# Twenty weight slabs split into their parts on ScalarE and VectorE instead of by a second transfer, and one activation table loaded at another place

## The chip, the cores and the metric

The kernel runs on one core of one Trainium2 chip, as one launch. The metric is the device time in microseconds (us) of one execution. A core has TensorE (PE, matrix products into PSUM), VectorE (DVE), ScalarE (ACT), GpSimd (POOL), SyncE (SP), and 16 DMA engines that move data between HBM and the on-chip SBUF. Each engine works through its own queue of instructions in the order in which the program wrote them; semaphores make one engine wait for another. Transfers are issued here from two queues, POOL's and SP's.

## The reference

Two layers of an encoder trunk on x of 512 tokens by 1024 features, all in float32:

```python
def reference(x, positions, attn_norm_g, w_in, ..., w_out, ffn_norm_g, w_gate, w_up, w_down):
    ...
    for l in range(DEPTH):                                   # DEPTH = 2
        h = rms_norm(x, attn_norm_g[l])
        z = jnp.einsum('bsd,dc->bsc', h, w_in[l])
        qa, ka, va, qb, kb, vb, ga, gb = jnp.split(z, IN_SPLITS, axis=-1)
        ...
        ya = jnp.einsum('bsc,cd->bsd', window_gqa(qa, ka, va, sink_a[l]), w_proj_a[l])
        ...
        yb = jnp.einsum('bsc,cd->bsd', neighbourhood_attn(qb, kb, vb, rel_bias_b[l]), w_proj_b[l])
        mixed = jax.nn.sigmoid(ga) * ya + jax.nn.sigmoid(gb) * yb
        x = x + jnp.einsum('bsd,de->bse', mixed, w_out[l])
        h = rms_norm(x, ffn_norm_g[l])
        u = jax.nn.silu(jnp.einsum('bsd,df->bsf', h, w_gate[l])) * jnp.einsum('bsd,df->bsf', h, w_up[l])
        x = x + jnp.einsum('bsf,fd->bsd', u, w_down[l])
    return x
```

w_out is 1024 by 1024, w_gate and w_up are 1024 by 2816.

## The kernel before

**Products in three parts.** A float32 operand is split into a high part in the reduced type `F32R` and a low part (what the rounding left). A product of two such operands takes three matrix products: high by high, high by low, low by high. Such a group of three with 512 columns is one unit of the program's own measure of progress (`UNIT`, L421); `pos` (L422) counts the progress of PE in it, and `at_pos` (L425) puts a piece of work at a position, where `tick` (L431) emits it between the matrix products.

**Weights** come in slabs. A slab of 512 rows by 256 columns lies on 128 partitions as 4 by 256 elements. `slab` (L443) books two steps for each: `w_load` (L504), 23 before its first use, a transfer on POOL's queue that rounds on the way and so leaves the high part; and `w_low` (L513), 15 before its use, where ACT writes the negated high part into the buffer of the low part and a second transfer from the same weights, also on POOL's queue, adds the weights onto it. `plan_pair` (L450) books the slabs of a pair of output blocks; `pair_matmul` (L798) takes them and runs the products.

**A layer** (`layer`, L1087) runs the input projections, 16 attention heads as chains of small steps between the products of the gates, the projections w_proj_a and w_proj_b (sigmoid gates before them), then w_out in four pairs, the leading 256 columns of w_gate and of w_up as one ordinary pair each, then five blocks ("quads") of 512 columns of w_gate and w_up by a Strassen scheme of seven products (m = 1, 5, 6, 2, 7, 3, 4), mixed with w_down.

**From w_out to the first quad.** `evac_x` (L1332) adds a finished block of w_out's product to x. After the second block of a pair it calls `Norm.chunk` (L763) for two blocks: on ACT the scaled high part and the square, on DVE the low part (`scalar_tensor_tensor`) and the running sum of squares. When the sum over all eight blocks is there, `Norm.chain` (L773) has PE sum it over the partitions (four tiny products with a vector of ones, "at<-ones" in the trace), DVE makes the inverse root (`rsqrt`, L744), PE spreads it ("at<-cst,rstd") and DVE copies it out as `rows`. `chain_x` (L1361) then scales x by it (eight `scalar_tensor_tensor`), makes the seven combinations of halves of x, and splits each: `high` on ACT, `low` on DVE. Meanwhile PE runs the leading pair of w_gate and of w_up, whose results are scaled by `rows`: `evac_g` (L1414) applies silu on ACT, `evac_u` (L1420) multiplies and splits. After the quad's products m = 1 and m = 5, product m = 6 goes on adding in a PSUM bank which `seed` (L1480) fills with the result of m = 1, by a copy on ACT (the trace's "ACT mm").

The quads' own weights are loaded raw, once, on SP's queue (`Quad.load`, L547), and split by ACT (`high`, L560) and DVE (`low`, L576); for the first w_gate quad most low parts are made by transfer (`low_by_transfer`, L533: ACT negates, a transfer adds).

**Who fixes the order.** The program is run twice. The first run is dry: it prices each instruction (`cost`, L274; DVE: elements by 1.04 or 0.52 ns and 0.075 us) and keeps a clock for each engine. A chain goes on when its `Need` (L355) is met by these clocks; `backlog` says how far the engine's clock may be ahead of PE's, and chain_x asks for 6.0 (`XLOG`, L34). The decisions and the places of all buffers in two arenas (one for float32, one for `F32R`) are kept, and the second run emits the program in that order. The dry run's clocks are no measurement; they set an order.

Of the kernel before, what the change touches and what calls it, by code (L numbers as in the profile page):

```python
# [12 lines left out]
F32 = mybir.dt.float32  # L13
F32R = mybir.dt.float32r
I32 = mybir.dt.int32
AF = mybir.ActivationFunctionType
ALU = mybir.AluOpType
AX = mybir.AxisListType

P = 128  # L20
# [5 lines left out]
KD = D // P  # L26
# [187 lines left out]
def trunk(ctx: ExitStack, tc: tile.TileContext, a: dict, out: bass.AP, lay: Layout):  # L214
# [20 lines left out]
    def buf(shape, dtype=F32):  # L235

        n = int(np.prod(shape))
        x = lay.place(n, dtype)
        t = arenas[dtype][:, x : x + n]
        if len(shape) == 2:  # L240
            t = t.rearrange("p (a b) -> p a b", b=shape[1])
        elif len(shape) == 3:
            t = t.rearrange("p (a b c) -> p a b c", b=shape[1], c=shape[2])
        return t
# [29 lines left out]
    def cost(eng, name, o, aps):  # L274
        n = max(x.free_size() for x in aps) / 1000.0
        in_psum = any(x.space == PS for x in aps[1:])
        if eng == "pe":
            cols = aps[2].free_size()
            if name == "transpose":
                return 0.1  # L280
            if aps[1].dtype == F32:
                return max(4 * cols, 256) / 2400.0 + 0.002
            return 0.12 if cols == 256 else (cols if cols >= 256 else 4 * cols) / 2255.0
        if eng == "act":
            return n * 0.833 + (0.06 if in_psum else 0.1) + 0.093 * sum(x.free_size() == 1 for x in aps[2:])
        if eng == "dve":
            fast = name in ("tensor_copy", "tensor_scalar") and not in_psum
            return n * (0.52 if fast else 6.4 if name == "reciprocal" else 1.04) + 0.075
        return n * 2.2 + 0.1

    steps = [0]
# [42 lines left out]
    V = Engine(nc.vector, "dve")  # L334
    A = Engine(nc.scalar, "act")
    G = Engine(nc.gpsimd, "pool")
    Q = Engine(nc.sync, "dma")
# [45 lines left out]
    def spawn(gen, after=None):  # L383
        c = [gen, Need()]
        if after is None:
            chains.append(c)
        else:
            chains.insert(chains.index(after) + 1, c)
        return c
# [32 lines left out]
    pos = [0.0]  # L422
    due = []

    def at_pos(t, f):  # L425
        bisect.insort(due, (t, len(seq), f))
        seq.append(0)

    seq = []

    def tick(dt):  # L431
        pos[0] += dt
        while due and due[0][0] <= pos[0]:
            due.pop(0)[2]()
# [3 lines left out]

    plan = []
    LEAD_H, LEAD_L, LEAD_RAW, LEAD_PREP = 23.0, 15.0, 14.0, 6.5  # L440
    total = [0.0]

    def slab(n, width, src, units, later_h=0.0, later_l=0.0):  # L443
        i = len(plan)
        plan.append((n, width, src))
        at_pos(total[0] - LEAD_H + later_h, lambda: w_load(i))
        at_pos(total[0] - LEAD_L + later_l, lambda: w_low(i))
        total[0] += units * UNIT

    def plan_pair(w, col, parts, row0=0):  # L450
        for k0 in range(0, parts, 4):
            n = min(4, parts - k0)
            r = row0 + P * k0
            slab(n, 256, [(0, w[r : r + P * n, col : col + 256])], 2 * n)

    def plan_token(w, cols):
        for k0 in range(0, KD, 2):
            at, src = 0, []
            for c, n in cols:
                src.append((at, w[P * k0 : P * k0 + 2 * P, c : c + n]))  # L460
                at += n
            slab(2, 512, src, 8)
# [6 lines left out]
    def ffn_steps():  # L469
        groups = [(0, 2)] + [(2 + 4 * i, 4) for i in range(QUADS)]  # L470
        steps = []
        for q in range(QUADS):
            ms = [("m", q, w, m) for w in ("w_gate", "w_up") for m in ORDER]
            ds = [("d", *groups[q], c) for c in range(KD)]
            for i, m in enumerate(ms):
                steps.append(m)
                if ds and i >= (1 if q else 5):
                    steps.append(ds.pop(0))
        return steps + [("d", *groups[-1], c) for c in range(KD)]
# [1 line left out]
    quads = {}  # L481

    def plan_ffn(l):
        plan_pair(a["w_gate"][l], 0, KD)
        plan_pair(a["w_up"][l], 0, KD)
        for step in ffn_steps():
            if step[0] == "m":
                _, q, w, m = step
                if m == ORDER[0]:
                    t = total[0]  # L490
                    early = 18.0 if q == 0 and w == "w_gate" else 0.0
                    quads[l, q, w] = Quad(a[w][l], 256 + 512 * q, t - early, early > 0.0)
                quads[l, q, w].due(m, total[0] - early)
                early = max(0.0, early - 1.2)
                total[0] += 24 * 0.12
            else:
                _, f0, n, c = step
                if c % 2 == 0:
                    slab(n, 256, [(0, a["w_down"][l][P * f0 : P * (f0 + n), P * c : P * c + 256])], 0, 3.0, 2.0)
                total[0] += n * UNIT  # L500

    highs, lows, used = {}, {}, [0]

    def w_load(i):  # L504

        if i not in highs:
            n1, n2, src = plan[i]
            highs[i] = buf([n1, n2], F32R)
            for at, ap in src:
                n = ap.shape[1]  # L510
                GQ.dma_start(highs[i][:, :, at : at + n], ap.rearrange("(k p) n -> p k n", p=P))

    def w_low(i):  # L513

        if i not in lows:
            n1, n2, src = plan[i]
            lows[i] = buf([n1, n2], F32R)
            A.activation(lows[i], highs[i].bitcast(F32), AF.Copy, scale=-1.0)
            for at, ap in src:
                n = ap.shape[1]  # L520
                GQ.dma_start(
                    lows[i][:, :, at : at + n], ap.rearrange("(k p) n -> p k n", p=P), accum_op=ALU.add
                )
# [61 lines left out]
    for l in range(DEPTH):  # L585
        w_in = a["w_in"][l]
        plan_token(w_in, [(QA0, 512)])
        plan_pair(w_in, KA0, KD)
        plan_token(w_in, [(QB0, 256), (KB0, 256)])
        plan_token(w_in, [(VB0, 512)])  # L590
        plan_token(w_in, [(QB0 + 256, 256), (KB0 + 256, 256)])
        for c in range(4):
            plan_pair(w_in, GA0 + 256 * c, KD)
        for c in range(ZB_AHEAD):
            plan_pair(w_in, GB0 + 256 * c, KD)
        for c in range(4):
            if c >= ZB_AHEAD:
                plan_pair(w_in, GB0 + 256 * c, KD)
            plan_pair(a["w_proj_a"][l], 256 * c, 4)
            plan_pair(a["w_proj_b"][l], 256 * c, 4)  # L600
        for c in range(4):
            plan_pair(a["w_out"][l], 256 * c, KD)
        plan_ffn(l)

    def gsplit(src, hi, lo, scale=None, eng=None):
# [26 lines left out]
    ones = cp.tile([P, 2], F32, tag="ones", name="ones")  # L632
# [4 lines left out]
    warm = cp.tile([P, 2], F32, tag="warm", name="warm")  # L637
# [449 lines left out]
    def layer(l):  # L1087
# [252 lines left out]


        last = l == DEPTH - 1
        spawn(nrm.chain())
        tail = []

# [87 lines left out]
        yield from pair_matmul(KD, nrm.xh, nrm.xl, evac_u)  # L1433

        gs = {}

        def soon(f, after=0.1):
            at_pos(pos[0] + after, f)

        def quadrant(q, w, i, t, src, sign):  # L1440

            if w == "w_gate":
                g = gs[i, t] = act()
                A.activation(g, src, AF.Silu, scale=sign)
                return
            hs, ls = us[q][i]
            g = gs[i, t]
            if sign > 0:
                V.tensor_tensor(g, src, g, ALU.mult)
            else:  # L1450
                V.scalar_tensor_tensor(g, src, sign, g, ALU.mult, ALU.mult)
            at = slice(256 * t, 256 * t + 256)
            g3 = g.rearrange("p (j n) -> p j n", j=2)
            A.copy(hs[:, :, at], g3)
            soon(lambda: V.tensor_tensor(ls[:, :, at], g3, hs[:, :, at].bitcast(F32), ALU.subtract), 1.0)
# [4 lines left out]
        def m_step(q, w, m):  # L1460
# [31 lines left out]
            def seed_c():  # L1492
                ps["c"] = plus(mm_bank())

            soon({
                1: seed,
                5: fetch,
# [34 lines left out]
        for i, step in enumerate(steps_[:-KD]):  # L1532
            if step[0] == "m":
                _, q, w, m = step
                yield f"x{l}{m}"
                yield from m_step(q, w, m)
            else:
                _, f0, n, c = step
                if c % 2 == 0:
                    wk = w_take()  # L1540
                o = mm_bank()
                yield from d_products(o, c, range(f0, f0 + n), wk, True, True)
                soon(lambda c=c, o=o: add_x(c, o))
        if not last:
            norms[2 * l + 2] = Norm(2 * l + 2)
        _, f0, n, _ = steps_[-1]
# [46 lines left out]
```

## Time and profile before

| what | value |
|---|---|
| median of 3 runs (lowest, highest) | 1441.97 us (1440.86, 1449.07) |
| the profiled execution | 1444.73 us |
| its span, first to last instruction | 1442.9 us |
| mean granted TensorE clock | 0.993 |
| ACT busy, DVE busy | 706.8 us, 912.2 us |
| moved by DMA | 221.10 MB |

The profile is of one execution. All instructions carry one line of the source (L308, the helper that emits them), so they are told apart by what they write and read: "mm" and "at" are PSUM banks, "arena" is any buffer of the two arenas, in_w_up and the like are the weights in HBM. A row of a timeline gives start, duration, engine, operation, operands and count; the bracket at its end is how long the engine stood idle before it, and what ended the wait. Rows of one kind that follow each other are merged; two such instructions on DVE or ACT overlap by some 0.1 us.

### The profile page before, as it was taken

To read this page: it belongs to the slowest core of one execution; us is meant where nothing else is said; L and a number is where in the kernel's file an instruction comes from. 1 tells how busy PE (TensorE), PEld (TensorE's weight loads), DVE (VectorE), ACT (ScalarE), POOL (GpSimd) and SP (SyncE) were. 2 spreads that over 40 slices of the span, in tenths; PEclk is the share of its full clock that TensorE was granted. 3 is DMA by queue.
4 is the path that set the end of the run, shared out by engine and by line. 5 is a ranking of instruction groups with operands and counts; after the bars stand their busy time and mean duration, and the time that the engine had idled before them with its cause. 6 is when DMAs were issued, how large, how long until landed. Compare 5 with 4: busy or idle time off the path is not lost.

```text
span 1442.9 us, 20988 instructions
## 1 busy us (share of the span) xinstructions
PE 1394.6 (97%) x8074; PEld 1224.6 (85%) x8074; DVE 912.2 (63%) x1752; ACT 706.8 (49%) x1191; POOL 363.4 (25%) x370
## 2 busy tenths in 40 slices
PE   5999999999989999999999999999998999999998
PEld 3778888888779999999987788888887999999997
DVE  3977777543667565665648768783448666574753
ACT  3476766643454343433544776574346343343431
POOL 4533222233221111101244322223232120111110
PEclk9999999999999999999999999999998999999999
DMA  9977788799865645645699678888996674736555
GB/s 226 170 159 129 140 161 157 142 196 259 146 139 144 156 117 143 155 112 117 134 201 174 132 129 155 160 158 155 260 206 109 147 175 116 178 89 145 121 100 117
DMA packets 209316, 221.10 MB, mean 153 GB/s; under 512 B 25900, under 2 KB 177632, under 8 KB 209216
## 3 DMA queue, kind: packets, MB, share of 16 engines
q0 software_dynamic: 157808, 165.13, 61.3%
q1 hardware_dynamic: 51408, 54.62, 13.3%
q8 instruction: 64, 1.05, 0.3%
q14 instruction: 36, 0.29, 0.1%
HBM read 207.13 MB, written 2.10 MB: 145 GB/s over the span
## 4 chain that ended last, share of the span: by engine, by line
PE 77%; DVE 12%; issue 3%; DMA 3%; ACT 3%; POOL 1%; DVEq 0%; POOLq 0%; ACTq 0%
PE mm L308 60%; PE at L308 18%; DVE arena L308 9%; ACT arena L308 3%; DVE sm L308 3%; DMA arena<-in_w_in 2%; DMA arena<-in_w_up 1%; POOL arena L308 1%; DMA cst<-in_consts 1%; DVE hf L308 0%; DVE den L308 0%; ACT L308 0%; ACT mm L308 0%; ACT sm L308 0%; DVEq L308 0%
## 5 line engine op out<-in xcount | busy, mean ns | idle before, releaser
L308 PE MATMUL mm<-arena 128*128 128x512 f32 (+1 forms) x5568 | 1123.6, 357 | 20.7 <-ACT mm L308 12.5
L308 PEld LDWEIGHTS mm<-arena 128*128 128x128 f32 x5568 | 907.1, 191 | 150.3 <-ACT mm L308 12.9
L308 ACT ACTIVATE arena<-arena 128x1024 fp32r<-128x1024 f32 (+3 forms) x276 | 232.7, 862 | 188.8 <-DMA arena<-in_w_down 58.9
L308 ACT CAST arena<-arena 128x1024 fp32r<-128x1024 f32 (+2 forms) x250 | 212.0, 864 | 220.9 <-DVE arena L308 218.5
L308 PE MATMUL at<-arena 128*128 128x256 f32 (+2 forms) x1952 | 303.8, 296 | 5.0 <-DVE arena L308 3.5
L308 PEld LDWEIGHTS at<-arena 128*128 128x128 f32 x1952 | 265.7, 191 | 25.9 <-DVE arena L308 8.1
L308 DVE TENSOR_TENSOR arena<-arena,arena 128x1024 fp32r<-128x1024 f32 (+2 forms) x240 | 233.0, 984 | 59.7 <-ACT arena L308 59.3
L308 DVE TENSOR_TENSOR arena<-arena,mm 128x512 f32<-128x512 f32 x144 | 98.7, 686 | 248.4 <-PE mm L308 248.3
L308 POOL DMA_DIRECT2D arena<-in_w_in x168 | 168.3, 1368 | 339.3 <-ACT arena L308 329.5
L308 POOL DMA_DIRECT2D arena<-in_w_down x96 | 98.2, 1218 | 502.1 <-ACT arena L308 357.5
L308 DVE TENSOR_TENSOR arena<-arena 128x1024 f32<-128x1024 f32 (+3 forms) x196 | 158.3, 823 | 4.0 <-ACT arena L308 1.5
L308 DVE TENSOR_TENSOR arena<-at,arena 128x384 fp32r<-128x384 f32 (+4 forms) x206 | 114.4, 562 | 49.6 <-ACT arena L308 42.2
L308 ACT CAST arena<-at 128x384 fp32r<-128x384 f32 (+2 forms) x164 | 74.4, 459 | 117.2 <-PE at L308 99.9
L308 PE MATMUL at<-cst,arena 128*128 128x128 f32 x504 | 85.9, 277 | 9.7 <-DVE arena L308 5.7
L308 PEld LDWEIGHTS at<-cst,arena 128*128 128x128 f32 x504 | 64.3, 142 | 26.8 <-DVE arena L308 6.8
L308 ACT ACTIVATE arena<-arena,negm 128x256 f32<-128x256 f32 (+1 forms) x128 | 71.4, 559 | 6.5 <-DVE negm L308 5.7
L308 DVE TENSOR_TENSOR arena<-mm,arena 128x512 f32<-128x512 f32 x72 | 49.3, 686 | 33.7 <-PE mm L308 33.6
L308 ACT COPY arena<-at 64x512 f32<-64x512 f32 (+1 forms) x60 | 34.9, 582 | 69.8 <-PE at L308 68.5
L308 POOL DMA_DIRECT2D arena<-in_w_out x32 | 35.1, 1287 | 60.5 <-ACT arena L308 60.5
L308 DVE CUSTOM_DVE_ANT_0 arena<-at,cst,nsnk 128x256 f32<-128x256 f32 (+1 forms) x64 | 34.4, 546 | 18.0 <-PE at L308 17.7
L308 DVE CUSTOM_DVE_ANT_0 arena<-at,arena 128x256 f32<-128x256 f32 (+1 forms) x64 | 30.7, 484 | 15.0 <-PE at L308 14.6
L308 DVE TENSOR_SCALAR arena<-arena,sm 128x384 f32<-128x384 f32 (+1 forms) x102 | 33.9, 387 | 1.1
(70 smaller groups left out, 436.4 us busy)
## 6 DMA issues: line engine op xcount, KB each, us to landing
arena<-in_w_in POOLq DMA_DIRECT2D x104, 512.0 KB, 7.2
arena<-in_w_down POOLq DMA_DIRECT2D x80, 512.0 KB, 6.7
arena<-in_w_gate SPq DMA_DIRECT2D x20, 1024.0 KB, 7.5
arena<-in_w_up SPq DMA_DIRECT2D x20, 1024.0 KB, 5.3
arena<-in_w_in POOLq DMA_DIRECT2D x64, 256.0 KB, 6.3
arena<-in_w_out POOLq DMA_DIRECT2D x32, 512.0 KB, 8.4
arena<-in_w_proj_a POOLq DMA_DIRECT2D x16, 512.0 KB, 7.0
arena<-in_w_proj_b POOLq DMA_DIRECT2D x16, 512.0 KB, 5.9
```

What stands on the lines that cost most here:

```text
L308: f(*args, **kw)
```

## The change

Three things change.

1. The 8 slabs of w_out and the 2 of the leading pair of w_gate, in each layer, are loaded raw, once, on SP's queue, 23 before their use (`w_raw`). 9 before the use, ACT copies the raw slab into the high part, and 1.2 later DVE subtracts the high part from the raw slab for the low part (`w_parts`).
2. Behind the last block of w_out, ACT applies silu to a two-element tile that nobody reads.
3. The dry run prices a DVE `scalar_tensor_tensor` with all operands in SBUF at 0.13 us plus its elements, where it had 0.075.

```diff
@@ cost
-            return n * (0.52 if fast else 6.4 if name == "reciprocal" else 1.04) + 0.075
+            per = 0.52 if fast else 6.4 if name == "reciprocal" else 1.04
+            return n * per + (0.13 if name == "scalar_tensor_tensor" and not in_psum else 0.075)
...
     LEAD_H, LEAD_L, LEAD_RAW, LEAD_PREP = 23.0, 15.0, 14.0, 6.5
+    LEAD_R, LEAD_P = 23.0, 9.0
...
-    def slab(n, width, src, units, later_h=0.0, later_l=0.0):
+    def slab(n, width, src, units, later_h=0.0, later_l=0.0, on_engines=False):
         i = len(plan)
         plan.append((n, width, src))
-        at_pos(total[0] - LEAD_H + later_h, lambda: w_load(i))
-        at_pos(total[0] - LEAD_L + later_l, lambda: w_low(i))
+        if on_engines:
+            at_pos(total[0] - LEAD_R, lambda: w_raw(i))
+            at_pos(total[0] - LEAD_P, lambda: w_parts(i))
+        else:
+            at_pos(total[0] - LEAD_H + later_h, lambda: w_load(i))
+            at_pos(total[0] - LEAD_L + later_l, lambda: w_low(i))
         total[0] += units * UNIT
...
     def plan_ffn(l):
-        plan_pair(a["w_gate"][l], 0, KD)
+        plan_pair(a["w_gate"][l], 0, KD, on_engines=True)
         plan_pair(a["w_up"][l], 0, KD)
...
+    def w_raw(i):
+
+        n1, n2, ((_, ap),) = plan[i]
+        raws[i] = buf([n1, n2])
+        Q.dma_start(raws[i], ap.rearrange("(k p) n -> p k n", p=P))
+
+    def w_parts(i):
+        n1, n2, _ = plan[i]
+        highs[i], lows[i] = buf([n1, n2], F32R), buf([n1, n2], F32R)
+        A.copy(highs[i], raws[i])
+        soon(lambda: V.tensor_tensor(lows[i], raws[i], highs[i].bitcast(F32), ALU.subtract), 1.2)
...
-            plan_pair(a["w_out"][l], 256 * c, KD)
+            plan_pair(a["w_out"][l], 256 * c, KD, on_engines=True)
...
         last = l == DEPTH - 1
+        A.activation(warm, ones, AF.Silu)
         spawn(nrm.chain())
```

`soon`, which puts a piece of work a little behind the present position, was a helper inside `layer` and is now one of `trunk`; `plan_pair` hands its keywords on to `slab`.

More of the change, by code (lines that the diff above doesn't have):

```diff
@@ L429, in trunk, with soon @@
     seq = []
+    def soon(f, after=0.1):
+        at_pos(pos[0] + after, f)
     def tick(dt):
@@ L440, in trunk, with plan_pair @@
     LEAD_H, LEAD_L, LEAD_RAW, LEAD_PREP = 23.0, 15.0, 14.0, 6.5
+    LEAD_R, LEAD_P = 23.0, 9.0
     total = [0.0]
-    def slab(n, width, src, units, later_h=0.0, later_l=0.0):
+    def slab(n, width, src, units, later_h=0.0, later_l=0.0, on_engines=False):
         i = len(plan)
         plan.append((n, width, src))
-        at_pos(total[0] - LEAD_H + later_h, lambda: w_load(i))
-        at_pos(total[0] - LEAD_L + later_l, lambda: w_low(i))
+        if on_engines:
[4 more added lines that the diff above has]
+            at_pos(total[0] - LEAD_L + later_l, lambda: w_low(i))
         total[0] += units * UNIT
-    def plan_pair(w, col, parts, row0=0):
+    def plan_pair(w, col, parts, row0=0, **kw):
         for k0 in range(0, parts, 4):
@@ L453, in plan_pair @@
             r = row0 + P * k0
-            slab(n, 256, [(0, w[r : r + P * n, col : col + 256])], 2 * n)
+            slab(n, 256, [(0, w[r : r + P * n, col : col + 256])], 2 * n, **kw)
     def plan_token(w, cols):
@@ L500, in plan_ffn @@
                 total[0] += n * UNIT
-    highs, lows, used = {}, {}, [0]
+    highs, lows, raws, used = {}, {}, {}, [0]
+    def w_raw(i):
[7 more added lines that the diff above has]
+        soon(lambda: V.tensor_tensor(lows[i], raws[i], highs[i].bitcast(F32), ALU.subtract), 1.2)
     def w_load(i):
@@ L1435, in layer @@
         gs = {}
-        def soon(f, after=0.1):
-            at_pos(pos[0] + after, f)
         def quadrant(q, w, i, t, src, sign):
```

## The prediction

> **What bounds the kernel now.** I read the page's busy shares first, then PE's waits, then the stretches around the longest ones, and last the timelines of PE, ACT and DVE there.
>
> ```profile
> PE 1394.6 (97%) x8074; PEld 1224.6 (85%) x8074; DVE 912.2 (63%) x1752; ACT 706.8 (49%) x1191; POOL 363.4 (25%) x370
> ```
>
> PE is busy for 1394.6 of 1442.9 us, and the change takes no product away. Whatever it is worth lies in the 48.3 us in which PE stands idle, and in time at a low clock. PE's own waits, longest sum first:
>
> ```profile
> PE mm L308 <- ACT mm L308: 12.5, 2, 6.3
> PE at L308 <- DVE arena L308: 11.5, 15, 2.3
> PE mm L308 <- DMA arena<-in_w_in: 8.3, 1, 8.3
> ```
>
> The third is the start of the program, which the change leaves as it is. The first is one wait in each layer, of over 6 us: product m = 6 of the first quad waits for ACT's seed. The second is fifteen small ones; its longest, 2.3, is the next row of interest. The stretches of layer 0 from w_out to the seed (PE, PEld, DVE, ACT, POOL busy, granted clock, DMA share, GB/s):
>
> ```profile
> 280.00:378.00 98.00, 98.00 (x434) 80.83 (x432) 38.81 (x58) 42.85 (x61) 33.94 (x33) 1.00 1.05 213
> 378.00:405.50 27.50, 25.11 (x138) 21.73 (x138) 25.94 (x43) 16.66 (x19) 5.43 (x5) 1.00 0.49 77
> 405.50:411.60 6.10, 0.00 (x0) 0.00 (x0) 4.66 (x7) 4.67 (x7) 1.27 (x1) 0.88 0.91 138
> 411.60:417.10 5.50, 5.49 (x26) 5.49 (x27) 0.28 (x1) 2.87 (x4) 3.20 (x3) 0.51 1.10 259
> ```
>
> In w_out's stage (to 378) PE never stops, while the DMA engines are more than full. From 378 on DVE is busy for 25.94 of 27.5 us: the stage hangs on DVE's row of work, and PE runs into it at 405.5. After that stall the granted clock is 0.51. PE in both layers:
>
> ```profile
> 380.33 1.02 PE L308 MATMUL at<-ones,arena 128*128 128x1 f32 x8 [2.34 <-DVE arena L308]
> 411.61 5.49 PE L308 MATMUL mm<-arena 128*128 128x256 f32 x24 [6.17 <-ACT mm L308]
> ```
> ```profile
> 1082.68 1.02 PE L308 MATMUL at<-ones,arena 128*128 128x1 f32 x8
> 1114.06 5.49 PE L308 MATMUL mm<-arena 128*128 128x256 f32 x24 [6.29 <-ACT mm L308]
> ```
>
> From the norm's small products to the end of the stall are 411.61 - 380.33 = 31.28 us in layer 0 and 1114.06 - 1082.68 = 31.38 in layer 1. The chain between them is the same in both, so what moves its start moves its end by as much. Layer 0 starts it 2.34 late; layer 1 not at all.
>
> Why 2.34 late is in ACT's queue (layer 0):
>
> ```profile
> 368.01 1.06 ACT L308 ACTIVATE arena<-arena 128x1024 fp32r<-128x1024 f32 x1 [2.96 <-DMA arena<-in_w_gate]
> 373.80 1.06 ACT L308 ACTIVATE arena<-arena 128x1024 fp32r<-128x1024 f32 x1 [4.73 <-DMA arena<-in_w_up]
> 374.77 1.03 ACT L308 CAST arena<-arena 128x1024 fp32r<-128x1024 f32 x1
> 375.71 0.72 ACT L308 ACTIVATE arena<-arena,vecT 128x512 fp32r<-128x512 f32 x1
> ```
> ```profile
> 362.89 1.26 POOL L308 DMA_DIRECT2D arena<-in_w_gate  x1 [1.62 <-ACT arena L308]
> 363.64 1.28 POOL L308 DMA_DIRECT2D arena<-in_w_up  x1
> 369.37 1.26 POOL L308 DMA_DIRECT2D arena<-in_w_gate  x1 [4.44 <-ACT arena L308]
> ```
> ```profile
> 363.64 10.09 DMA arena<-in_w_up
> ```
> ```profile
> 375.83 1.22 DVE L308 TENSOR_TENSOR arena<-arena,arena 128x1024 fp32r<-128x1024 f32 x1 [3.91 <-ACT arena L308]
> 376.98 0.68 DVE L308 TENSOR_TENSOR arena<-arena,mm 128x512 f32<-128x512 f32 x1
> ```
>
> ACT stands for 4.73 us before the negation of w_up's first slab, whose transfer took 10.09 us. POOL issued it only at 363.64, right behind w_gate's second transfer, which had itself waited for ACT's negation; POOL, in order, carries every lateness on to the next slab. Behind the blocked ACT wait the quad's cast (374.77), DVE's subtraction (375.83), and behind that, in DVE's order, the last `evac_x` (376.98) and with it the sum of squares that PE needs at 378.
>
> **The change part by part.** The slabs first.
>
> ```profile
> L308 POOL DMA_DIRECT2D arena<-in_w_out x32 | 35.1, 1287 | 60.5 <-ACT arena L308 60.5
> L308 ACT ACTIVATE arena<-arena 128x1024 fp32r<-128x1024 f32 x158 | 166.9, 1057 | 150.4 <-DMA arena<-in_w_down 56.8 <-DMA arena<-in_w_out 44.9 <-DMA arena<-in_w_in 13.0
> L308 ACT CAST arena<-arena 128x1024 fp32r<-128x1024 f32 x154 | 158.2, 1045 | 136.0 <-DVE arena L308 133.7 <-PE at L308 2.2
> L308 DVE TENSOR_TENSOR arena<-arena,arena 128x1024 fp32r<-128x1024 f32 x144 | 174.6, 1220 | 35.6 <-ACT arena L308 35.4
> ```
>
> Twenty slabs (16 of w_out, 4 of w_gate) lose two POOL transfers each and gain one on SP: 40 issues of about 1.29 us, 51 us, leave POOL, and 20 x 512 KB = 10.5 MB of 221.10 are not moved. ACT gives 20 x 1.057 and takes 20 x 1.045: nothing. DVE takes 20 x 1.22 = 24.4 us more. Per layer nine of its ten subtractions fall before the last evac_x pair, under PE's 98 us, where DVE has 98.00 - 38.81 = 59 idle: price nothing, with a cover of 59 for 11. Without cover each would cost 1.22.
>
> The tenth, of w_gate's second slab, is due 7.8 before its use, which is 5.4 after w_out's end E; on the grid of units it is emitted at about E - 2.0. DVE then has: the first evac_x from E - 2.7 (0.69), this 1.22, the quad's 1.22, the second evac_x from E + 0.3, and four of about 0.65 for the last two chunks: done at E + 3.7. The norm's products stand 18 products behind E, at E + 4.1 (373.9 + 4.1 = 378.0, where PE stopped). It fits by 0.4; if not, the rest is lost on PE one for one.
>
> POOL has nothing of w_out or w_gate to wait for now, so w_up's two transfers are issued at their place or ahead of it, into a quieter DMA. ACT's 4.73 goes, and with it layer 0's 2.34. What is late next:
>
> ```profile
> arena<-in_w_up POOLq DMA_DIRECT2D x8, 512.0 KB, 7.1
> ```
>
> w_up's first transfer is planned at E - 12.1 = 361.8 and its negation at E - 4.1 = 369.8. At the median of 7.1 it lands at 368.9, before ACT asks; at the 10.09 of the crowded stage it would land at 371.9, still 1.8 earlier than now. Bounds: 0 (the transfer is still late) to 2.34; I take **2.34**, because the reason for the lateness is the queue that empties. In layer 1 PE did not wait here, so the same repair is worth 0.
>
> The raw transfers meet SP's queue, in order with the quads' raw loads; these are wanted later, and nothing in SP's queue waits for ACT. I price that at nothing; the cover is 14 planned us from issue to cast.
>
> Then silu's table:
>
> ```profile
> 396.41 1.05 ACT L308 CAST arena<-arena 128x1024 fp32r<-128x1024 f32 x1 [2.98 <-DVE arena L308]
> 397.48 1.28 ACT L308 ACT_TABLE_LOAD   x1
> 398.78 1.15 ACT L308 ACTIVATE arena<-arena 128x512 f32<-128x512 f32 x2
> 399.84 1.98 ACT L308 CAST arena<-arena 128x1024 fp32r<-128x1024 f32 x2
> 401.72 1.06 ACT L308 ACTIVATE arena<-arena 128x1024 fp32r<-128x1024 f32 x1
> ```
> ```profile
> 397.50 3.48 DVE L308 TENSOR_TENSOR arena<-arena,arena 128x1024 fp32r<-128x1024 f32 x3
> 401.85 1.22 DVE L308 TENSOR_TENSOR arena<-arena,arena 128x1024 fp32r<-128x1024 f32 x1 [0.87 <-ACT arena L308]
> ```
>
> Without the load ACT is 398.78 - 397.48 = 1.30 earlier, but DVE is busy to 400.98 and waits only 0.87 for the second of the two casts. So 0.87 a layer is the upper end. The load itself goes behind the last chunk's square, where ACT waits before its next cast in either layer (1.55 us in layer 0); uncovered, 1.3 would fall on a quad's cast that nothing needs for 15 us.
>
> The third edit decides how much of 0.87 comes. I followed the dry run by its own prices: between the norm and the splitting of x stand seventeen of the re-priced instructions (8 in rsqrt, 8 scalings, 1 difference), 17 x 0.055 = 0.94 on DVE's planned clock. The step that emits the second of the two casts above sat within chain_x's limit of 6.0; with 0.94 more it is 0.13 beyond it and comes two units later, behind the 1.06 negation of the row at 401.72. Then the cast ends at 397.48 + 1.06 + 0.98 + 0.98 + 1.05 = 401.55 and DVE goes on at 401.57: a gain of 0.28. Ends 0.28 and 0.87; I take **0.28**, since the count says so, though by a margin of 0.13.
>
> Does the slow clock go too? The stall is then 6.17 - 0.28 = 5.9 us, and 24 products after it take 5.49 us against 2.87 at full clock:
>
> ```profile
> 416.90 3.07 PE L308 MATMUL at<-arena 128*128 128x256 f32 x24
> 419.98 11.41 PE mm L308 x84
> 431.38 2.87 PE at L308 x24
> ```
>
> So each stall costs 2.62 more than its length. An idle time of 2.34 left the clock at 1.00 (378 to 405.5), one of 6.17 did not; 5.9 is near the second. Bounds 0 to 2.62 a layer; I take 0. [...]
>
> Everywhere else the new price may re-order steps of the attention chains. The trace before can't show it; bounds are the waits there, 11.5 - 2.34 = 9.2 us, all gone or doubled; I take 0.
>
> **Sum.** 2.34 + 0.28 + 0.28 = 2.9 us off the profiled execution's 1444.73: 1441.8. That execution was 2.76 above the median of the runs, so for the median 1441.97 - 2.9 = **1439.1 us**, own range 1437 to 1441.
>
> **The rivals.**
>
> *The stall breaks.* If DVE's chain gains more than I see (0.87 in each layer, the norm earlier) and the idle time falls to where the clock holds, both layers gain 2.62 as well: 1439.1 - 1.2 - 5.2 = 1432.7. For it: the one threshold lies somewhere between 2.34 and 6.17. Against it: 31.3 us of which DVE works nearly all. Chance 0.12.
>
> *Layer 0 stays late.* The tenth subtraction, the table load and w_up's negation all stand before the norm's sum; the fit is 0.4, and in the dry run the norm's place holds by 0.02 of a unit's 0.68. If it slips a unit, 0.68 is lost in each layer; if the transfer stays late, 2.34 is not won. The time is then 1441.4, no change. Chance 0.20.
>
> *Slower: a new order in the attention.* The dearer scalar_tensor_tensor shifts the dry run's clocks in the rope tables, the norms and rsqrt, and the chains of sixteen heads are interleaved by comparisons of these clocks. Nothing in the trace says that the new order fits better. If it adds 60% to the 9.2 us of small waits, 5.5 us, the time is 1444.6. It decides from 2.9 us of new waits on, a third more than there are. For it: PE's waits are spread over fifteen places, each under 1 us save the 2.34, a sign of an order that already fits. [...] Chance 0.18.
>
> **How the numbers follow.** Forecast 0.50, the three rivals 0.12, 0.20 and 0.18. The range runs from the first rival with a third of the attention's waits gone as well (1432.7 - 3 = 1430) to the slower one with a doubling nearly whole (1439.1 + 8 = 1447): 1430 to 1447. A measurement of this kernel tells about 1% from no change, 14.4 us. Faster than 1427.5 would need nearly all of 2.34 + 12.5 for the stalls and 5.2 for the clock: 0.05. Slower than 1456.4 needs a new wait of 17 us, such as ACT blocked on a raw slab in every pair: 0.04. Within 1%: 0.91.
>
> **What would show it.** Right: the wait of the "at<-ones" products in layer 0 gone; no ACT wait on in_w_up near E - 4; ACT_TABLE_LOAD directly behind a 128x512 square some 20 us earlier, still 8 of them; DVE's 0.87 wait shrunk to about 0.6; 31.28 down to 31.0; stalls on "ACT mm" of about 5.9 and a granted clock near 0.5 behind both; POOL with 40 issues less, 210.6 MB moved. Wrong: ACT or PE waiting for a raw in_w_out or in_w_gate; a stall under 5 us or a full clock behind it; waits of PE on DVE in the attention that sum to over 12 us.

## The result, and the profile after

The changed kernel takes 1433.55 us (median of 7, 1432.72 to 1434.49); the kernel before, run beside it, 1444.48 (7 runs). The ratio is 0.9925, with a 95% interval of 0.9908 to 0.9942: 10.9 us less, 8 to 13 by the interval. The forecast was 1439.1, within 1430 to 1447, and 2.9 us less. The time fell into the range; the gain is almost four times what was forecast. Of the two experiments with prices of 0.09 and 0.11 below, one execution each ran at a granted clock of 0.56 and 0.66 (2310 and 1965 us) and is in no ratio and no median here.

The profiled execution after has a span of 1431.2 us against 1442.9, so 11.7 us can be traced. The page's busy line and the DMA total:

```profile
PE 1392.1 (97%) x8074; PEld 1223.6 (85%) x8074; DVE 936.3 (65%) x1768; ACT 708.1 (49%) x1197; POOL 323.4 (23%) x330
...
DMA packets 198756, 210.61 MB, mean 147 GB/s; under 512 B 25580, under 2 KB 167072, under 8 KB 198656
```

DVE has 24.1 us more work, ACT the same, POOL 40 issues less, and 10.5 MB less are moved: these were forecast. PE's busy time is the same to 2.5 us, so the gain lies in its waits:

```profile
PE mm L309 <- ACT mm L309: 10.6, 2, 5.3
PE mm L309 <- DMA arena<-in_w_in: 6.9, 1, 6.9
...
PE at L309 <- DVE arena L309: 6.0, 12, 1.5
```

Fifteen waits on DVE with 11.5 us are now twelve with 6.0. The longest, 2.3 before the norm of layer 0, is gone, and of the others 9.2 became 6.0. The waits for the seed went from 12.5 to 10.6. PE at the norm and behind the stall, in both layers:

```profile
375.61 0.94 PE L309 MATMUL at<-ones,arena 128*128 128x1 f32 x8
...
405.95 5.15 PE L309 MATMUL mm<-arena 128*128 128x256 f32 x24 [5.31 <-ACT mm L309]
```
```profile
1073.71 0.95 PE L309 MATMUL at<-ones,arena 128*128 128x1 f32 x8
...
1104.03 4.38 PE L309 MATMUL mm<-arena 128*128 128x256 f32 x24 [5.29 <-ACT mm L309]
```

From the norm to the end of the stall are 30.34 and 30.32 us, where 31.28 and 31.38 were. The starts of the "at<-ones" rows (each layer has two norms; those at 44.05 and 734.48 before and at 43.48 and 728.48 after open the layers) and of the products behind the stall cut the span into stretches:

| stretch | before, us | after, us | difference |
|---|---|---|---|
| start to the first norm | 44.05 | 43.48 | -0.57 |
| layer 0, norm to norm (attention to w_out) | 336.28 | 332.13 | -4.15 |
| layer 0, norm to the end of the stall | 31.28 | 30.34 | -0.94 |
| layer 0, from there to layer 1's first norm | 322.87 | 322.53 | -0.34 |
| layer 1, norm to norm | 348.20 | 345.23 | -2.97 |
| layer 1, norm to the end of the stall | 31.38 | 30.32 | -1.06 |
| layer 1, from there to the end | 328.84 | 327.17 | -1.67 |

The sum is -11.70. Of the 4.15 in layer 0, 2.34 are the wait that was forecast; 1.81 there and 2.97 in layer 1 are not.

The DMA side in w_out's stage, and the stall with the time behind it (columns as in the prediction):

```profile
280.00:378.00 98.00, 98.00 (x438) 81.26 (x437) 54.05 (x79) 47.08 (x66) 14.82 (x14) 1.00 0.66 159
...
400.60:405.90 5.30, 0.04 (x1) 0.00 (x0) 3.84 (x6) 3.87 (x7) 1.28 (x1) 0.80 0.83 208
405.90:410.90 5.00, 4.95 (x24) 4.96 (x25) 0.31 (x1) 2.91 (x4) 3.25 (x3) 0.53 1.19 224
```

The DMA share fell from 1.05 to 0.66, and DVE's busy time rose from 38.8 to 54.1 without PE stopping: the subtractions did lie under PE. POOL issued both of w_up's transfers together at 350.15, 11 us and more before the place of 363.64 and 370.12 that they had:

```profile
350.15 1.58 POOL L309 DMA_DIRECT2D arena<-in_w_up  x2 [39.12 <-PE mm L309]
365.02 1.30 POOL L309 DMA_DIRECT2D arena<-in_w_up  x1 [13.29 <-ACT arena L309]
```

ACT and DVE around silu's table:

```profile
373.23 0.61 ACT L309 ACTIVATE arena<-arena 128x512 f32<-128x512 f32 x1
373.87 1.28 ACT L309 ACT_TABLE_LOAD   x1
375.16 0.20 ACT L309 ACTIVATE warm<-ones 128x2 f32<-128x2 f32 x1
...
392.60 1.15 ACT L309 ACTIVATE arena<-arena 128x512 f32<-128x512 f32 x2
393.65 1.04 ACT L309 CAST arena<-arena 128x1024 fp32r<-128x1024 f32 x1
394.72 1.06 ACT L309 ACTIVATE arena<-arena 128x1024 fp32r<-128x1024 f32 x1
395.68 1.03 ACT L309 CAST arena<-arena 128x1024 fp32r<-128x1024 f32 x1
```
```profile
392.72 3.48 DVE L309 TENSOR_TENSOR arena<-arena,arena 128x1024 fp32r<-128x1024 f32 x3
396.13 1.22 DVE L309 TENSOR_TENSOR arena<-arena 128x1024 f32<-128x1024 f32 x1
397.26 1.21 DVE L309 TENSOR_TENSOR arena<-arena,arena 128x1024 fp32r<-128x1024 f32 x1
```

The load is where the forecast had it. The negation (394.72) did slip between the two casts, as worked out. But DVE doesn't wait for the second cast: a sum or difference for the quad (396.13) now stands ahead of the subtraction (397.26). The dry run, which priced the later cast as well, had moved the subtraction too. The forecast followed ACT's order and left DVE's as it was.

### The profile page after: what moved, and what is told of

Same layout as the page of the kernel before. It is cut to its first block, busy times and chain, and to the rows that moved or that the text cites. A ratio compares the mean times of both kernels' runs of the same rounds, so it can differ in the third digit from the quotient of the medians.

```text
span 1431.2 us, 20961 instructions
## 1 busy us (share of the span) xinstructions
PE 1392.1 (97%) x8074; PEld 1223.6 (85%) x8074; DVE 936.3 (65%) x1768; ACT 708.1 (49%) x1197; POOL 323.4 (23%) x330
## 3 DMA queue, kind: packets, MB, share of 16 engines
q8 instruction: 64, 1.05, 0.3%
## 4 chain that ended last, share of the span: by engine, by line
PE 85%; DVE 10%; issue 2%; ACT 2%; DMA 1%; POOL 0%; DVEq 0%; ACTq 0%; POOLq 0%
PE mm L309 65%; PE at L309 20%; DVE arena L309 7%; DVE sm L309 3%; ACT arena L309 1%; DMA arena<-in_w_in 1%; DMA cst<-in_consts 1%; POOL arena L309 0%; DVE hf L309 0%; ACT L309 0%; ACT mm L309 0%; DVE den L309 0%; ACT sm L309 0%; DVEq L1607 0%; DVE rstd L309 0%
## 5 line engine op out<-in xcount | busy, mean ns | idle before, releaser
L309 PE MATMUL mm<-arena 128*128 128x512 f32 (+1 forms) x5568 | 1124.4, 357 | 17.5 <-ACT mm L309 10.6
L309 ACT CAST arena<-arena 128x1024 fp32r<-128x1024 f32 (+2 forms) x270 | 231.1, 878 | 232.8 <-DVE arena L309 226.0
L309 DVE TENSOR_TENSOR arena<-arena,arena 128x1024 fp32r<-128x1024 f32 (+2 forms) x260 | 256.7, 1003 | 51.5 <-ACT arena L309 51.0
L309 ACT ACTIVATE arena<-arena 128x1024 fp32r<-128x1024 f32 (+3 forms) x256 | 211.0, 846 | 125.5 <-DMA arena<-in_w_down 62.6
L309 DVE TENSOR_TENSOR arena<-arena 128x1024 f32<-128x1024 f32 (+4 forms) x196 | 158.7, 823 | 4.0 <-ACT arena L309 1.5
L309 ACT ACTIVATE arena<-arena,vecT 128x512 fp32r<-128x512 f32 x24 | 17.4, 726 | 54.6 <-DVE arena L309 54.2
L309 POOL DMA_DIRECT2D arena<-in_w_up x8 | 8.2, 1031 | 125.8 <-PE mm L309 78.1
```

What stands on the lines that cost most here:

```text
L309: f(*args, **kw)
```

## The experiments

There are two theories about the 8 us that were not forecast: the new price re-ordered the attention's steps, or the freed queues and DMA helped there. If it is the price, a second question is whether a truer price makes a better order or just another one. Then comes the stall itself: an order, or an amount of work. Ratios are to the kernel before, in the same round of runs, with 95% intervals; microseconds "by the ratio" are what it lacks to 1, times the time of the kernel before.

**Silu's table alone.**

```diff
         last = l == DEPTH - 1
+        A.activation(warm, ones, AF.Silu)
```

> The kernel before with the second edit alone (silu's table loaded behind w_out). The order of PE and DVE is that of before. Theory A (the table's place is worth DVE's wait of 0.87 us a layer): from the norm's products to the end of the stall 30.4 us instead of 31.3 in both layers, the wait of 0.87 gone, layer 0's wait of 2.34 still there; about 1.7 us less in all, up to 3 if the shorter stall also keeps some of the clock. Rival (the gain of 0.94 and 1.06 seen after all three edits comes from the new order of ACT and DVE that the price makes, not from the table): 31.0 or more in both layers, 0 to 0.6 us less.

1441.49 us, ratio 0.9985 (0.9974 to 0.9997): 2.2 us less by the ratio, 1.2 by the medians.

```profile
380.94 1.02 PE L308 MATMUL at<-ones,arena 128*128 128x1 f32 x8 [2.65 <-DVE arena L308]
...
411.28 4.42 PE L308 MATMUL mm<-arena 128*128 128x256 f32 x24 [5.29 <-ACT mm L308]
```
```profile
398.12 4.62 DVE L308 TENSOR_TENSOR arena<-arena,arena 128x1024 fp32r<-128x1024 f32 x4
```

30.34 us from norm to stall's end in layer 0 and 30.28 in layer 1, with the old order of DVE and PE: the table's place alone gives the whole 0.94 and 1.1. DVE now runs the four subtractions without a pause, where it waited 0.87 ahead of the last. The wait before the norm stayed. Theory A holds for this edit.

**The price alone.**

```diff
-            return n * (0.52 if fast else 6.4 if name == "reciprocal" else 1.04) + 0.075
+            per = 0.52 if fast else 6.4 if name == "reciprocal" else 1.04
+            return n * per + (0.13 if name == "scalar_tensor_tensor" and not in_psum else 0.075)
```

> The kernel before with the third edit alone (the dry run's price of scalar_tensor_tensor). Theory A (this edit alone re-orders PE's work in the attention, and that is where 3 to 4 us came from): PE's waits on DVE there fall from 9.2 us to about 6, time 3 to 5 us less, layer 0's wait of 2.34 before the norm's products stays, as does the place of the table load. Rival (the attention's gain comes from fewer bytes and freer queues, so from the slabs): 0, within 1 us of before.

1435.76 us, ratio 0.9944 (0.9930 to 0.9958): 8 us less by the ratio, 6.9 by the medians. An edit that adds and removes no instruction is worth more than either of the other two. Layer 1 from norm to norm takes 345.45 (348.20 before), layer 0 331.69 (336.28). PE's waits on DVE are 5.8 us in eleven. Two things were expected otherwise: the gain, 3 to 5 us, and the wait before layer 0's norm:

```profile
374.92 0.94 PE L309 MATMUL at<-ones,arena 128*128 128x1 f32 x8
...
406.15 4.57 PE L309 MATMUL mm<-arena 128*128 128x256 f32 x24 [6.20 <-ACT mm L309]
```
```profile
367.44 1.06 ACT L309 ACTIVATE arena<-arena 128x1024 fp32r<-128x1024 f32 x1 [3.10 <-DMA arena<-in_w_up]
```

It is gone too, though ACT still waits 3.10 for w_up. The negation now runs 3.4 us ahead of w_out's end, where it was 0.1: the lateness is still there, but no longer long enough to reach PE.

**The slabs alone,** with `w_raw` and `w_parts` as in the change.

```diff
     def plan_ffn(l):
-        plan_pair(a["w_gate"][l], 0, KD)
+        plan_pair(a["w_gate"][l], 0, KD, on_engines=True)
...
-            plan_pair(a["w_out"][l], 256 * c, KD)
+            plan_pair(a["w_out"][l], 256 * c, KD, on_engines=True)
```

> The kernel before with the first edit alone (the twenty slabs raw on SP, split by ACT and DVE). PE's order is that of before. Theory A: the wait of 2.34 us in layer 0 goes, ACT waits nowhere for in_w_up before the norm, from the norm's products to the end of the stall 31.3 us as before in both layers; 2.3 us less in all. Rival (the slabs also bring what was gained in the attention): 5 us less or more.

1441.29 us, ratio 0.9984 (0.9974 to 0.9995): 2.3 us less by the ratio, 1.4 by the medians. The time alone can't confirm a size of 2.34; the trace shows that the wait itself is gone:

```profile
378.13 0.95 PE L308 MATMUL at<-ones,arena 128*128 128x1 f32 x8
...
409.47 5.49 PE L308 MATMUL mm<-arena 128*128 128x256 f32 x24 [6.31 <-ACT mm L308]
```

No wait at the norm, 31.34 us behind it, and layer 1 from norm to norm 348.37 as before (348.20). The rival falls: in the old order, a freer DMA did nothing for the attention.

**The slabs and the table, without the price** (the diffs of the slabs and of silu's table together).

> The first and second edit without the third. Theory A (the parts add up): layer 0's 2.34 gone, 30.4 us from the norm to the end of the stall in both layers, PE's order in the attention that of before with its waits of about 9 us; 4.1 us less than before, so 5 to 6 us slower than with all three edits. Rival (the price is worth nothing): the time of all three edits, 10 us less than before.

1438.38 us, ratio 0.9959 (0.9945 to 0.9972): 5.9 us less by the ratio, 4.3 by the medians. From norm to stall's end 30.37 and 30.36; layer 1 from norm to norm 348.16. The parts add up here; the price is missing in the attention.

**The price and the table, without the slabs** (the diffs of the price and of silu's table together).

> The second and third edit without the first (the slabs as before, by two transfers on POOL). Theory A (the parts overlap: the new order alone has already taken away layer 0's wait of 2.34 us, so the slabs have nothing left to win): within 1 us of all three edits, about 1433 to 1435. Rival (the slabs are worth their 2 us whatever the order): 2 us or more slower than all three edits, 1435.5 or more.

1435.10 us, ratio 0.9935 (0.9914 to 0.9955), against 0.9925 (0.9908 to 0.9942) with the slabs. The intervals overlap; 1.4 us between them can't be told from nothing, and the time lies between what the two theories asked for.

```profile
375.57 0.95 PE L309 MATMUL at<-ones,arena 128*128 128x1 f32 x8
...
406.22 5.35 PE L309 MATMUL mm<-arena 128*128 128x256 f32 x24 [5.57 <-ACT mm L309]
```

No wait at the norm here either; from there to the end of the stall it takes 30.65 us, and 30.34 with the slabs. The slabs' 2.34 and the price's new order remove the same wait, so the edit that the change is named after has little or nothing left to give beside the others.

**Other prices.** The kernel before with the price alone, at 0.09, 0.11 and 0.17 instead of 0.13.

```diff
-            return n * per + (0.13 if name == "scalar_tensor_tensor" and not in_psum else 0.075)
+            return n * per + (0.09 if name == "scalar_tensor_tensor" and not in_psum else 0.075)
```

> The kernel before with the price alone, at 0.09 instead of 0.13. Theory A (a truer price makes a better order in the attention, and the trace's short scalar_tensor_tensor take 0.16 to 0.19 us): part of what 0.13 gave, 1 to 4 us less than before. Rival (any new price draws a new order, and the orders scatter): no trend over 0.075, 0.09, 0.11, 0.13 and 0.17; this one anywhere from 8 us less to 5 us more.

> The kernel before with the price alone, at 0.11. Theory A (truer is better): between 0.09 and 0.13, 3 to 7 us less than before. Rival (a draw): anywhere from 8 us less to 5 us more, out of line with its neighbours by more than 2 us.

> The kernel before with the price alone, at 0.17, near the 0.16 that the shortest scalar_tensor_tensor takes in the trace. Theory A (truer is better): at least as much as 0.13 gave, 7 to 9 us less. Rival (a draw): less than half of that, or slower than before.

All three are slower than before: 1446.74 us at 0.09 (ratio 1.0020, 1.0006 to 1.0033), 1447.24 at 0.11 (1.0020, 1.0007 to 1.0032), 1445.89 at 0.17 (1.0024, 1.0009 to 1.0040). PE's waits at 0.09, then at 0.17:

```profile
PE at L309 <- DVE arena L309: 15.2, 18, 3.6
PE mm L309 <- ACT mm L309: 10.0, 2, 5.0
```
```profile
PE mm L309 <- ACT mm L309: 12.2, 2, 6.5
PE at L309 <- DVE arena L309: 14.6, 14, 2.4
```

| price, us | 0.075 (before) | 0.09 | 0.11 | 0.13 | 0.17 |
|---|---|---|---|---|---|
| layer 0, norm to norm | 336.28 | 339.45 | 337.43 | 331.69 | 335.53 |
| layer 1, norm to norm | 348.20 | 349.14 | 350.01 | 345.45 | 350.12 |
| ratio | 1 | 1.0020 | 1.0020 | 0.9944 | 1.0024 |

There is no trend. Each price draws another order of the heads' steps; of five, 0.13 has the good one. That the price is truer is not what makes the time. A new price also moves buffers in the arenas; no run separates that from the order.

**The stall: put evac_u off by 7,** on top of all three edits.

```diff
-        yield from pair_matmul(KD, nrm.xh, nrm.xl, evac_u)
+        yield from pair_matmul(KD, nrm.xh, nrm.xl, lambda j, ps: soon(lambda: evac_u(j, ps), 7.0))
```

> All three edits, and evac_u (scaling, gating and splitting of the leading pair's result) put off by 7 of planned PE progress, so that ACT's seed copy for product m = 6 stands ahead of the two splits. Theory A (the stall of 5.3 us is ACT's order: the seed, whose input is in PSUM from 397.7 on, waits behind two splits whose inputs DVE has not reached; DVE has time to catch up later): the wait of PE on ACT's seed falls from 5.3 us to under 1 in both layers, the half clock behind it goes, and 10 to 14 us go in all, if no other product of the quad stalls in its place. Rival (DVE's work as such is the bound, so the stall moves to a later product): PE waits of 4 us or more at products m = 2, 7 or 3 and under 3 us less in all.

1433.15 us, ratio 0.9928 (0.9914 to 0.9943): nothing gained.

```profile
402.71 4.63 PE L309 MATMUL mm<-arena 128*128 128x256 f32 x24 [2.59 <-ACT mm L309]
...
411.74 11.66 PE L309 MATMUL mm<-arena 128*128 128x256 f32 x84 [1.52 <-DVE mm L309]
```

The wait for the seed halved, a wait of 1.52 on DVE (seed_c, behind the second half of evac_u) took part of it back, and the clock dropped behind 2.59 us of idleness as well (the granted clock was 0.62 from 402.7 to 405.0 and 0.65 from there to 407.4). Neither theory's numbers came.

**Put off by 12,** so that both halves come behind seed_c: the same diff with 12.0.

> As the run that put evac_u off by 7, but by 12, so that both of its halves come behind seed_c too. Theory A (putting it off by 7 gave back what it won because the second half fell between the seed and seed_c on DVE): the wait of 1.52 us on DVE goes, the wait on ACT's seed stays at 1 to 2.6 because ACT still works off two casts and a negation for the quad's last products first; 2 to 4 us less than with all three edits. Rival (DVE's work as such is the bound): another wait of about the same sum of 4 us at products 2, 7 or 3, no gain over the three edits.

1428.20 us, ratio 0.9909 (0.9892 to 0.9926).

```profile
403.36 4.64 PE L309 MATMUL mm<-arena 128*128 128x256 f32 x24 [2.64 <-ACT mm L309]
...
410.71 1.48 PE L309 MATMUL mm<-arena 128*128 128x256 f32 x11
```
```profile
408.10 0.70 DVE L309 TENSOR_TENSOR mm<-mm,arena 128x512 f32<-128x512 f32 x1 [6.02 <-PE mm L309]
```

The second wait is gone, the first stays at 2.64, as theory A had it. DVE stands idle for 6.02 us ahead of seed_c, so its work as such is not the bound here.

**Products 3 and 4 prepared later,** by DVE, on top of that.

```diff
-                early = max(0.0, early - 1.2)
+                early = min(6.0, early) if m == 7 else max(0.0, early - 1.2)
...
-            if self.by_transfer and m not in (1, 2):
+            if self.by_transfer and m not in (1, 2, 3, 4):
```

> As before it, and the first w_gate quad's parts for products 3 and 4 are made later (6 instead of some 12 ahead of the usual place) and their low parts by DVE instead of by transfer, so that their casts come behind the seed on ACT and the sum for product 3 behind it on DVE. Theory A (the stall is an order, not an amount of work): PE waits under 0.6 us for the seed in both layers, the clock stays at full behind it, 8 to 13 us less than with all three edits, about 1421 to 1426. Rival (DVE is the bound): 3 us or more of waits at products 7, 3 or 4, less than 4 us gained.

1424.84 us, ratio 0.9883 (0.9868 to 0.9898), 17 us less than before: the fastest median of all. Yet the wait is 2.33, not under 0.6. ACT shows why:

```profile
398.69 3.07 ACT L309 CAST arena<-arena 128x1024 fp32r<-128x1024 f32 x3 [2.48 <-DVE arena L309]
401.79 0.57 ACT L309 COPY mm<-at 128x512 f32<-128x512 f32 x1
```

Three casts, the first of which waits 2.48 for DVE, still stand ahead of the seed (401.79), whose input was ready from 397.1 on.

**The seed ahead of these casts,** on top of that; only ACT's order changes.

```diff
             yield from low(2)
+            yield Need(keys=[f"seed{l}"])
             V.tensor_tensor(b12, b22, b12, ALU.subtract)
...
                 A.copy(ps["b"], o)
+                done.add(f"seed{l}")
```

> As the run with products 3 and 4 made later, and chain_x does not go on to its seventh and third combination before the seed is emitted; only ACT's order changes, by the seed standing ahead of two or three casts that wait for DVE. Theory A (the 2.33 us left are the seed behind the casts at 398.69): PE's wait for the seed is gone or under 0.3 us in both layers, no half clock, 5 to 8 us less than the run before it, 1417 to 1420. Rival (PE then meets DVE at the next product): 2 us or more of waits at products 2, 7 or 3, under 3 us gained.

1425.76 us, ratio 0.9871 (0.9851 to 0.9891): no difference from the run before it that can be told.

```profile
401.60 3.14 PE L309 MATMUL mm<-arena 128*128 128x256 f32 x24 [0.30 <-ACT mm L309]
...
408.91 6.72 PE L309 MATMUL mm<-arena 128*128 128x256 f32 x51 [1.29 <-DVE mm L309]
```

The seed's wait is 0.30 and the clock holds (those 24 products took 3.14 us and 3.13 in layer 1, and the run's mean granted clock is 1.0), but 1.29 on DVE and three waits of 0.2 to 0.4 follow. The 1.29 is not an amount of DVE's work, for DVE is idle ahead of the addition that PE waits for:

```profile
406.08 1.05 ACT L309 CAST arena<-arena 128x1024 fp32r<-128x1024 f32 x1 [2.62 <-DVE arena L309]
407.03 0.62 ACT L309 ACTIVATE arena<-arena 128x512 fp32r<-128x512 f32 x1
407.56 0.57 ACT L309 COPY arena<-at 128x512 f32<-128x512 f32 x1
```
```profile
408.16 0.70 DVE L309 TENSOR_TENSOR mm<-mm,arena 128x512 f32<-128x512 f32 x1 [2.12 <-ACT arena L309]
```

DVE's addition (seed_c) waits 2.12 for an ACT copy of m = 5's result (407.56), which PE had finished at 401.3; ACT waits 2.62 for DVE ahead of a cast that stands before that copy. It is ACT's order once more; no run moved this copy. By the ratios some 6 us were won of the stalls and the slow clock behind them (0.9925 to 0.9883), by re-ordering and not by less work for DVE, which was even given more (939.8 us against 936.3). What the waits that are left would give way to isn't shown.

## Why the prediction was right and wrong

**The bound, right.** PE's busy time was 1394.6 us before and 1392.1 after, and the gain came out of its waits and the clock. That the time fell into the range is in part luck: the sum's own 1437 to 1441 was missed by 3.5 us, and only the wide range covered a term that was put at 0. The first rival's 1432.7 comes within 1 us of the measured time, but by stalls that break, and these stayed at 5.3 us.

**The slabs: 2.34, right as a size, incomplete as a cause.** The slabs alone gave 2.3 us by the ratio, by the mechanism of the forecast (the POOL queue empties, w_up is there in time). POOL's share was over-stated: 51 us were to leave it, a count of instructions times their mean, and 40.0 left its busy time; the row that was shown has 32 issues in 35.1 us, since they overlap. The forecast did not see that the same wait would also fall to a new order: by the price alone it went as well, so the two don't add.

**Silu's table: 0.28 taken, 0.94 and 1.06 measured.** The step that failed is "comes two units later, behind the 1.06 negation": it happened on ACT, but the subtraction that waits for that cast was moved as well. The upper end of 0.87 was the right one. In layer 0 the 0.07 beyond it is the overlap of two DVE instructions that follow each other without a wait; 0.12 more in layer 1 I can't place.

**"Everywhere else the new price may re-order steps ... I take 0": the term that failed.** It was 1.8 us in layer 0 and 3.0 in layer 1. The bounds given, 9.2 us gone or doubled, held: between the norms 3.3 us of idleness went, besides the 2.34, and 1.5 that the profile counts as busy. The 9.2 itself was not all attention, nor were all of these waits under 1 us: one of 1.47 us is at the end of the program, before and after. Zero was a fair middle for a draw, and of the four prices tried 0.13 alone won by it; but its spread was the largest unknown and stood last.

**The clock: 0 taken, some 1.8 in the profile** (0.34 behind layer 0's stall, 1.4 of the 1.67 behind layer 1's). It is not a price per stall. By the clock records of the two traces the granted clock was 0.50 for 6.83 and 10.24 us in the two layers before, and for 6.83 and 3.41 after. Over all the runs the 24 products behind the stall took 4.57 to 5.49 us at stalls of 6.17 to 6.45 us, 4.37 to 5.49 at 4.98 to 5.78, 3.13 to 4.65 at 2.32 to 2.64, and 3.14 and 3.13 at 0.30 and 0.29. So a shorter stall does help, but its length alone does not set the price: behind 5.29 and 5.26 us in the two layers of silu's table alone, the 24 products took 4.42 and 5.49.

**The rivals.** "Slower: a new order in the attention" named the right place and the wrong sign for this price; at 0.09, 0.11 and 0.17 it is what happened. "Layer 0 stays late" did not come: PE no longer waits before that norm. "The stall breaks" did not come with the change; further re-ordering brought some 6 us of it.

## What to carry to other kernels

Where a planner's prices decide the order of a program, changing a price is a draw of a new order: measure several before believing that one is better because it is truer, and undo it by itself before crediting the edit that it came with. A wait at the end of a chain of queues can be removed from either end, so edits that cure the same wait don't add. When PE waits for a small copy, look at what stands ahead of it on its engine and what that waits for; here 2 to 4 us of other engines' lateness were queued in front of 0.57 us of work.

## What the runs showed of the hardware

The clock can drop after less idleness than the prediction took, and not each time. The kernel with products 3 and 4 prepared later idled 2.33 and 2.32 us ahead of the same 24 products in its two layers; columns as before, with the granted clock third from the end:

```profile
402.42 4.45 PE L309 MATMUL mm<-arena 128*128 128x256 f32 x24 [2.33 <-ACT mm L309]
```
```profile
400.36:403.77 3.41, 1.35 (x11) 1.35 (x12) 3.41 (x4) 1.98 (x3) 0.00 (x0) 1.00 0.52 102
403.77:407.18 3.41, 3.41 (x18) 3.41 (x18) 0.85 (x2) 2.74 (x4) 0.86 (x2) 0.50 0.00 0
...
1093.26:1096.68 3.42, 1.58 (x14) 1.38 (x12) 3.38 (x4) 3.19 (x4) 0.00 (x0) 1.00 1.17 184
1096.68:1100.09 3.41, 2.93 (x24) 2.93 (x25) 2.48 (x3) 1.32 (x2) 0.00 (x0) 1.00 0.03 5
```

In layer 0 the clock was at 0.50 for 3.41 us, in layer 1 it stayed at 1.00 (those 24 products took 3.13 us). In layer 0 PE was idle for 2.06 of the 3.41 us ahead of the slow stretch; in layer 1 it was idle for 1.84 of the 3.42 us up to 1096.68 and for 0.48 of the 3.41 from there. With evac_u put off by 7 the clock dropped behind 2.59 us; in the kernel before it stayed at 1.00 behind the 2.34 at layer 0's norm. So no one idle time between 2.34 and 6.17, as the first rival had it, parts the waits with a drop from those without: 2.33 had one. What decides between the two, no run shows.
